# Attention in a two-layer trunk: the denominators' selection issued three steps later, and a buffer of its own for the transposed values

## The chip, the core and the metric

The kernel runs on one core of a Trainium2 chip. The metric is the device time of one execution in microseconds, lower is better; given is the median of three runs. One execution was also taken by the hardware profiler. Engines are named as in the profile: PE (TensorE, matmuls and transposes; PEld its weight loads), DVE (VectorE), ACT (ScalarE), POOL (GpSimd), SP (the queue that issues DMAs).

## What is computed

A trunk of two layers on 512 tokens of width 1024: a retention layer, then a layer of dilated attention, each followed by a gated MLP. The change lies in the attention layer. It has 16 heads of dimension 64 in three groups with (window, dilation) of (128, 1), (512, 4) and (2048, 16). Each group has its own queries, keys and values, and the groups' outputs are merged by their softmax denominators:

```python
s = jnp.where(valid, einsum('bqhd,bkhd->bhqk', qb, kb) * scale, -inf)
m = jnp.max(s, axis=-1, keepdims=True)
p = jnp.exp(s - m)
den = jnp.sum(p, axis=-1)
o = einsum('bhqk,bkhd->bqhd', p, vb) / den
lse = m[..., 0] + jnp.log(den)
...
alpha = softmax(stack(lses), axis=0)          # over the three groups
o = einsum('gbsh,gbshd->bshd', alpha, stack(outs))
```

Because the groups are merged by these weights, the kernel adds up the unnormalised outputs of all groups under one common maximum and divides once by the sum of all denominators.

## The kernel before

**Projections.** Keys, queries and values are projected in fp32 split into a high and a low part, three matmuls for each product (`mm3`, lines 208 to 210). Each projection of 128 columns (`rotated` for keys and queries, `residue_values` for the values of groups 1 and 2, `values` for those of group 0) is a Python generator. It yields after every `mm3` of its eight, so one *step* is three matmuls of 512 columns. Weights are fetched by SP into `raw`, scaled by a gain on POOL (L158), split by ACT (`whi`, L168) and DVE (`wlo`, L169).

**Heads.** `heads(hp, ...)` treats two heads at a time, so there are eight *pairs* (hp = 0 to 7). A query block of 128 rows has an index rb: 0 to 3 are the four blocks of group 0 in token order, 4 to 7 the four residues modulo 4 that serve groups 1 and 2. The stages are:

- scores in two halves (L756, `sc`): rb 0 to 3 with group 0, then rb 4 to 7 with groups 1 and 2; DVE adds the mask and takes row maxima (L760, `p` and `mst`);
- two *selections*, which bring the row maxima of the residue order into token order and back;
- exponentials with row sums `den` on ACT (L822);
- `weights(i, rb)`, steps i = 0 to 7 in the order rb = 4, 5, 6, 7, 0, 1, 2, 3, two at a time: PE transposes `p` into a bank of PSUM (`pt`, L846), and DVE for even i (L852) or ACT for odd i (L850) copies it out as `pT`. At i = 4 the first four are applied to the values (`apply`, L866, into `po`) ahead of the transposes of steps 4 and 5;
- a third selection, that of the denominators, and from it `inv`: one over the sum of all denominators, which ACT spreads (L885) and PE transposes (L895) to scale the output `o` (L896).

A selection is two functions. `select` spreads its source on DVE (L778, `spread`) and multiplies it by a 0/1 matrix on PE (L785, `pz`, 128x32, into a PSUM bank). `gather` reads `pz` on DVE (L790, `z`) and reduces it (L795); for the third selection a sum (L882) and a reciprocal (L883) follow.

**PSUM banks.** Tag "tr" has two banks, in turn used by half of the score tiles, by every `pt` and by `pz`. An instruction that writes into a bank waits until the tile that had it before is read. In the steps around the third selection the order of the tiles in "tr" is: `pt` of steps 2 and 3, `pz`, `pt` of steps 4, 5, 6 and 7, the output's `pt`.

**Order on the engines.** `_weave` drives a pair's `heads` generator, and at each of its `yield`s lets the filling generators (the next pair's projections) go on by 3.7 steps (hp 0, 1, 3, 5) or 2.95 (hp 2, 4, 6). PE's order is that of the program there (`manual_schedule`); the other engines' order is the scheduler's. The last pair (hp = 7) is woven with the output projection at one step per `yield`, and there PE's order is also the scheduler's.

**Residue values.** `residue_values` projects a value tile as 128 columns by 512 tokens; ACT copies it out in residue order to `vT` (L674), PE transposes it by residue (L693), and ACT copies the result to `vr` (L694). The transposes are issued some steps later (`transpose_pending`). `vT` is allocated under the tag "sh" with one buffer. The same tag and buffer serve `rotated` as scratch: DVE shuffles a projection into it (L714), POOL multiplies it (L717, L721) and adds it to the rotated tile `m` (L718, L722), which is a key or query tile of the next scores.

Of the kernel before, what the change touches and what calls it, by code (L numbers as in the profile page):

```python
# [10 lines left out]
F32 = mybir.dt.float32  # L11
# [6 lines left out]
P = 128  # L18
SEQ = 512
# [77 lines left out]
def trunk(ctx: ExitStack, tc: tile.TileContext, a, out):  # L97
# [95 lines left out]
    def cols_unit(w, n0, nt=1, k0=0, gain=None):  # L193
        return unit(cols_of(w, n0, nt, k0), gain)
# [11 lines left out]
    def mm3(o, l, r, start, stop):  # L206

        nc.tensor.matmul(o, lhsT=l[0], rhs=r[0], start=start, stop=False)  # L208
        nc.tensor.matmul(o, lhsT=l[0], rhs=r[1], start=False, stop=False)  # L209
        nc.tensor.matmul(o, lhsT=l[1], rhs=r[0], start=False, stop=stop)  # L210
# [402 lines left out]
    def attention(pool, post, then, late, ahead):  # L613
# [5 lines left out]
        def by_residue(t):  # L619
            return t.rearrange("p (q r) -> p r q", r=4)  # L620

        def in_runs(t):
            return t.rearrange("p (r q) -> p r q", r=4)

        with pool as tmp:
# [37 lines left out]
            def residue_values(hp, g, res):  # L663


                pm = ps.tile([P, 512], F32, name="pm", tag="mm", bufs=4)
                wu = cols_unit(w_kv, 3 * D + g * D + hp * P, gain=g_kv)
                for k in range(KT):
                    mm3(pm, [t[:, blk(k)] for t in wu], (hi[:, k, :], lo[:, k, :]), k == 0, k == KT - 1)
                    aged(k)  # L670
                    if k < KT - 1:
                        yield
                vT = tmp.tile([P, SEQ], F32, name="vT", tag="sh", bufs=1)
                nc.scalar.copy(out=in_runs(vT), in_=by_residue(pm))  # L674
                v = rtiles[hp % 2 * 2 + g - 1]
                pending.append([vT, v, 0])
                res.append(v)
                yield

            def aged(k):  # L680

                for t in pending:
                    t[2] += 1
                if k == 6:
                    transpose_pending(0)
# [45 lines left out]
            def heads(hp, ks, qs, vs, vr, res):  # L731
# [43 lines left out]
                def select(src, m_in, mat):  # L775

                    spread = small.tile([P, 4, 8], F32, name="spread", tag="spread", bufs=2)
                    nc.vector.tensor_mul(  # L778
                        out=spread,
                        in0=src.unsqueeze(1).broadcast_to([P, 4, 8]),  # L780
                        in1=m_in.unsqueeze(2).broadcast_to([P, 4, 8]),
                    )
                    pz = ps.tile([P, 512], F32, name="pz", tag="tr")
                    spread = spread.rearrange("p i c -> p (i c)")
                    nc.tensor.matmul(pz[:, 0:32], lhsT=mat, rhs=spread, start=True, stop=True)  # L785
                    return pz
# [47 lines left out]
                def weights(i, rb):  # L834


                    if rb < 4:
                        src = [sc[rb][:, :, 0:P] if rb == 0 else sc[rb][:, :, P:]]
                        if rb < 3:
                            src.append(sc[rb + 1][:, :, 0:P])  # L840
                    else:
                        src = [sc[rb][:, :, 0:P], sc[rb][:, :, P:]]
                    pt = ps.tile([P, 2, 2, P], F32, name="pt", tag="tr")
                    for h in range(2):
                        for n, p in enumerate(src):
                            nc.tensor.transpose(out=pt[:, h, n, :], in_=p[:, h, :], identity=ident)  # L846
                    pT = tmp.tile([P, 2, 2, P], F32, name="pT", tag="pT", bufs=6)
                    n = len(src)
                    if i % 2:
                        nc.scalar.copy(out=pT[:, :, 0:n, :], in_=pt[:, :, 0:n, :])  # L850
                    else:
                        nc.vector.tensor_copy(out=pT[:, :, 0:n, :], in_=pt[:, :, 0:n, :])  # L852
                    return pT, n

                def apply(i, rb, pT, n):

                    for g in range(1 if rb < 4 else 2):
                        for h in range(2):
                            hs = slice(h * HD, (h + 1) * HD)
                            if rb < 4:  # L860
                                v, p = vs[rb][:, hp % 2, hs], pT[:, h, 0:n, :].rearrange("p n q -> p (n q)")
                                dst = po[hs, rb * P : (rb + n) * P]
                            else:
                                v, p = vr[g][:, rb - 4, hs], pT[:, h, g, :]
                                dst = row_cols(po[hs, :], rb)
                            nc.tensor.matmul(dst, lhsT=v, rhs=p, start=i == 0 and g == 0, stop=i == 7)  # L866
# [3 lines left out]
                for i in range(0, 8, 2):  # L870
                    if i == 4:
                        for t in prev:
                            apply(*t)
                    prev += [(j, order[j], *weights(j, order[j])) for j in (i, i + 1)]
                    if i == 2:
                        pz = select(den[:, 8:16], quarter, sel[:, 0:128])
                    yield
                    yield

                inv = small.tile([P, 8], F32, name="inv", tag="inv", bufs=2)  # L880
# [50 lines left out]
            for hp in range(last + 1):  # L931
                att = heads(hp, *kq[hp], vs[hp // 2], vr[hp], o)
                if hp == last:
                    _weave(att, wo, 1)
                    _run(wo)
                    break

                fill = [residue_values(hp + 1, g, vr[hp + 1]) for g in (1, 2)] + [keys_queries(hp + 1, *kq[hp + 1])]
                if hp == 0:
                    fill = [residue_values(0, g, vr[0]) for g in (1, 2)] + fill  # L940
                if hp % 2 == 1:
                    fill.append(values(hp // 2 + 1, vs[hp // 2 + 1]))
                fill = chain(*fill)
                with tc.manual_schedule(engines={E.PE}):
                    _weave(att, fill, 3.7 if hp % 2 or hp == 0 else 2.95)
                    _run(fill)
                if hp == last - 1:
                    for _ in range(6):
                        next(wo)
# [65 lines left out]
```

## Time and profile before

| | |
|---|---|
| time, median of three runs | 1747.56 us (1743.99 to 1750.2) |
| the profiled execution's own time | 1750.31 us |
| its span in the profile | 1748.5 us |
| mean granted clock of PE | 0.991 |
| HBM read, written | 152.62 MB, 2.10 MB |
| heads and their fill, 845 to 1347 us: PE, DVE, ACT, POOL busy | 487.65, 284.95, 184.42, 265.16 of 502 us |

Times in the profile count from the start of the span. A timeline's row has start, duration, engine, line, operation, the tiles as out<-in, the shape, a count, and in brackets how long the engine had been idle and what released it. Matmuls are pipelined, so their rows overlap: the distance of two starts is what one costs. In the table of waits stand the instruction that waited, what it waited for, the total, the number of times and the longest. The row of a window has, in this order, its bounds, its length, the busy time and the number of instructions (in brackets) of PE, PEld, DVE, ACT and POOL, the granted clock of PE, the busy share of the DMA engines and GB/s.

### The profile page before, as it was taken

Reading aid. Unit: us, or ns where it says so; the run is one execution under the profiler, and the core shown is the slowest. Engines: PE = TensorE matmul, PEld = TensorE weight load, DVE = VectorE, ACT = ScalarE, POOL = GpSimd, SP = SyncE. Lnnn points to the kernel's source line nnn. Section 1 sums busy time; section 2 is a strip of 40 time slices with the busy share of each in tenths; the row PEclk is TensorE's granted clock in tenths of the full one; section 3 lists DMA queues with packets and bytes.
Section 4 is the critical chain, followed back from the end, with each engine's and each line's share of the span. In section 5 each row is a group of like instructions: output and inputs, shape, how many; then the busy total and the mean of one; then the engine's idle time right before and its main releaser. Section 6 shows DMA issues by size and latency. Waiting matters only on the chain.

```text
span 1748.5 us, 21650 instructions
## 1 busy us (share of the span) xinstructions
PE 1709.0 (98%) x8590; PEld 1417.3 (81%) x8590; DVE 939.2 (54%) x1461; ACT 613.3 (35%) x1076; POOL 397.5 (23%) x284
## 2 busy tenths in 40 slices
PE   9999999999999999999899999999999999999998
PEld 6888888887888888878778888878887788888886
DVE  4553545468544544557546556556455754454454
ACT  5232422325442422423144243244245544233241
POOL 1000000005000000046665656566431400000003
PEclk9999999999999999999999999999999999999999
DMA  6422333214332332432222222222221333233231
GB/s 211 125 67 84 91 97 91 85 36 109 121 96 73 121 96 73 133 106 61 85 71 64 85 73 81 68 70 85 69 73 44 87 116 97 83 111 96 84 109 49
DMA packets 202162, 156.10 MB, mean 89 GB/s; under 512 B 4989, under 2 KB 182093, under 8 KB 202062
## 3 DMA queue, kind: packets, MB, share of 16 engines
q1 hardware_dynamic: 202062, 154.73, 28.9%
q8 instruction: 67, 1.10, 0.3%
q14 instruction: 33, 0.27, 0.0%
HBM read 152.62 MB, written 2.10 MB: 88 GB/s over the span
## 4 chain that ended last, share of the span: by engine, by line
PE 89%; DVE 5%; POOL 3%; ACT 1%; issue 1%; DMA 1%; POOLq 0%; SPq 0%; DVEq 0%; ACTq 0%
PE pm L208 20%; PE pm L210 20%; PE pm L209 20%; PE po L208 6%; PE po L209 6%; PE po L210 6%; PE sc L756 2%; DVE wlo L169 2%; PE po L866 2%; PE pt L846 1%; DVE x L305 1%; PE s L450 1%; PE pt L264 1%; DVE h L256 1%; POOL raw L158 1%
## 5 line engine op out<-in xcount | busy, mean ns | idle before, releaser
L208 PE MATMUL pm<-hT_hi,whi 128*128 128x512 f32 (+1 forms) x1424 | 546.3, 384 | 0.0
L209 PE MATMUL pm<-hT_lo,whi 128*128 128x512 f32 (+1 forms) x1424 | 540.0, 379 | 0.3 <-DVE hT_lo L199 0.3
L210 PE MATMUL pm<-hT_hi,wlo 128*128 128x512 f32 (+1 forms) x1424 | 539.7, 379 | 0.0
L169 DVE TENSOR_TENSOR wlo<-raw,whi 128x1024 fp32r<-128x1024 f32 x275 | 377.7, 1378 | 299.9 <-ACT whi L168 296.2
L168 ACT CAST whi<-raw 128x1024 fp32r<-128x1024 f32 x275 | 286.0, 1051 | 650.0 <-PE pm L209 355.3
L208 PEld LDWEIGHTS pm<-hT_hi,whi 128*128 128x128 f32 x1424 | 269.6, 189 | 51.5 <-issue 3.2
L210 PEld LDWEIGHTS pm<-hT_hi,wlo 128*128 128x128 f32 x1424 | 269.3, 189 | 50.1
L209 PEld LDWEIGHTS pm<-hT_lo,whi 128*128 128x128 f32 x1424 | 269.6, 189 | 48.5 <-DVE hT_lo L199 1.2
L158 POOL TENSOR_TENSOR raw<-raw,cols 128x1024 f32<-128x1024 f32 x72 | 140.7, 1957 | 465.8 <-DMA raw<-in_att_w_kv 385.6
L271 DVE TENSOR_TENSOR m<-po,m 128x512 f32<-128x512 f32 x112 | 77.1, 688 | 139.0 <-PE po L210 138.8
L208 PE MATMUL pm<-whi,hT_hi 128*128 128x512 f32 (+1 forms) x384 | 142.2, 370 | 0.0
L323 POOL TENSOR_TENSOR h<-m,gain 128x512 f32<-128x512 f32 x31 | 47.4, 1528 | 407.7 <-DVE m L271 407.2
L208 PE MATMUL po<-whi,ah 128*128 128x512 f32 x352 | 137.9, 392 | 0.0
L209 PE MATMUL po<-wlo,ah 128*128 128x512 f32 x352 | 137.9, 392 | 0.0
L210 PE MATMUL po<-whi,al 128*128 128x512 f32 x352 | 137.8, 391 | 0.0
L210 PE MATMUL pm<-whi,hT_lo 128*128 128x512 f32 (+1 forms) x384 | 136.9, 356 | 0.0
L209 PE MATMUL pm<-wlo,hT_hi 128*128 128x512 f32 (+1 forms) x384 | 136.7, 356 | 0.0
L215 POOL TENSOR_TENSOR r_gn<-v_gn,nhalf 128x1 f32<-128x1 f32 x16 | 8.8, 548 | 357.4 <-DVE v_gn L480 357.4
L208 PEld LDWEIGHTS pm<-whi,hT_hi 128*128 128x128 f32 x384 | 73.0, 190 | 11.5 <-issue 1.0
L209 PEld LDWEIGHTS pm<-wlo,hT_hi 128*128 128x128 f32 x384 | 73.1, 190 | 10.8 <-DVE wlo L169 0.6
L210 PEld LDWEIGHTS pm<-whi,hT_lo 128*128 128x128 f32 x384 | 72.8, 190 | 10.7 <-DVE hT_lo L199 0.3
L208 PEld LDWEIGHTS po<-whi,ah 128*128 128x128 f32 x352 | 66.5, 189 | 14.2 <-DVE m L271 0.4
(137 smaller groups left out, 1959.8 us busy)
## 6 DMA issues: line engine op xcount, KB each, us to landing
raw<-in_ffn_w_up SPq DMA_DIRECT2D x88, 512.0 KB, 3.8
raw<-in_att_w_kv SPq DMA_DIRECT2D x48, 512.0 KB, 4.0
raw<-in_ret_w_in SPq DMA_DIRECT2D x47, 512.0 KB, 3.9
raw<-in_ffn_w_down SPq DMA_DIRECT2D x44, 512.0 KB, 3.2
raw<-in_att_w_q SPq DMA_DIRECT2D x24, 512.0 KB, 3.7
raw<-in_ret_w_out SPq DMA_DIRECT2D x16, 512.0 KB, 3.3
raw<-in_att_w_o SPq DMA_DIRECT2D x8, 512.0 KB, 3.3
x<-in_x SPq DMA_DIRECT2D x3, 512.0 KB, 6.6
```

The source lines that it names most:

```text
L158: nc.gpsimd.tensor_mul(out=dst, in0=dst, in1=gain.unsqueeze(2).broadcast_to(list(src.shape)))
L168: nc.scalar.copy(out=hi, in_=raw)
L169: nc.vector.tensor_sub(out=lo, in0=raw, in1=hi.bitcast(F32))
L208: nc.tensor.matmul(o, lhsT=l[0], rhs=r[0], start=start, stop=False)
L209: nc.tensor.matmul(o, lhsT=l[0], rhs=r[1], start=False, stop=False)
L210: nc.tensor.matmul(o, lhsT=l[1], rhs=r[0], start=False, stop=stop)
L256: nc.vector.scalar_tensor_tensor(out=h, in0=x[b][:, half(c)], scalar=r, in1=gain[c], op0=ALU.mult, op1=ALU.mult)
L264: nc.tensor.transpose(out=pt[:, j, :], in_=hs[c][:, blk(j)], identity=ident)
L271: nc.vector.tensor_add(out=dst, in0=src, in1=dst)
L323: eng.tensor_mul(out=mg[b][c], in0=m[b][:, half(c)], in1=gain[:, half(c)])
L756: nc.tensor.matmul(pm[h][:, i, c], lhsT=q, rhs=k, start=True, stop=True)
L866: nc.tensor.matmul(dst, lhsT=v, rhs=p, start=i == 0 and g == 0, stop=i == 7)
```

## The change

```diff
                 # residue_values
-                vT = tmp.tile([P, SEQ], F32, name="vT", tag="sh", bufs=1)
+                vT = tmp.tile([P, SEQ], F32, name="vT", tag="vT", bufs=1)
                 nc.scalar.copy(out=in_runs(vT), in_=by_residue(pm))
...
                 # heads, the loop over i in range(0, 8, 2)
                     prev += [(j, order[j], *weights(j, order[j])) for j in (i, i + 1)]
-                    if i == 2:
+                    yield
+                    if i == 4:
                         pz = select(den[:, 8:16], quarter, sel[:, 0:128])
-                    yield
                     yield
```

The selection of the denominators is issued at i = 4, after one of the two `yield`s, instead of at i = 2 ahead of both: three `yield`s later. In "tr" the order of tiles becomes `pt` of steps 2, 3, 4 and 5, `pz`, `pt` of steps 6 and 7. `vT` gets 2 KB per partition of its own; the order on ACT, POOL and SP is the same as before. ACT's copy into `vT` then no longer waits for POOL (in before, the first `vT` of hp 0, 1, 3 and 5 did).

On PE, in the first pair, the selection leaves the place behind the transposes of steps 2 and 3 and goes to one behind those of steps 4 and 5. The difference against before:

```order
@@ -3840,5 +3840,4 @@
 L210 MATMUL pm<-hT_hi,wlo 128x512
 L846 MATMUL pt<-ident,p 128x128 x8
-L785 MATMUL pz<-spread,sel 128x32
 L208 MATMUL pm<-hT_hi,whi 128x512
 L209 MATMUL pm<-hT_lo,whi 128x512
@@ -3883,4 +3882,5 @@
 L209 MATMUL pm<-hT_lo,whi 128x512
 L210 MATMUL pm<-hT_hi,wlo 128x512
+L785 MATMUL pz<-spread,sel 128x32
 L208 MATMUL pm<-hT_hi,whi 128x512
 L209 MATMUL pm<-hT_lo,whi 128x512
```

In between lie eight steps, `apply` for the first four tiles, the transposes of steps 4 and 5, and three steps; the next transposes, those of step 6, come three or four steps behind the new place (six in hp 1, 3 and 5). The same holds in hp 1 to 6, with six steps in place of the eight in hp 2, 4 and 6. In the last pair the selection goes behind the transposes of steps 4 and 5 and two matmuls.

On DVE, the reading of `pz` and what follows from it move behind the copy of step 4 (the first L852 below). In hp 2, 4 and 6 they also move behind the handling of a finished projection (L714, L716) and a weight's low part (L169):

```order
+L852 COPY pT<-pt 128x512
+L714 STREAM_SHUFFLE sh<-pm 128x512
+L716 TENSOR_TENSOR m_79<-pm,rope 128x512
+L169 TENSOR_TENSOR wlo<-raw,whi 128x1024
 L790 TENSOR_TENSOR z<-pz,sel 128x32
 L795 TENSOR_REDUCE inv<-z 128x8
 L882 TENSOR_TENSOR inv<-inv,den 128x8
 L883 RECIPROCAL inv<-inv 128x8
-L852 COPY pT<-pt 128x512
-L714 STREAM_SHUFFLE sh<-pm 128x512
-L716 TENSOR_TENSOR m_79<-pm,rope 128x512
-L169 TENSOR_TENSOR wlo<-raw,whi 128x1024
```

In hp 0, 1, 3 and 5 they stand directly behind the copy of step 4.

## The prediction

> **What bounds the kernel now.** I read the page first, then who waited for whom on PE, then the places of these waits in the timeline, and the granted clock around them. In the page's part 1, a column is an engine's busy time and its share of the span; its part 4 gives the shares of the chain that ended last. The table of waits has the waiting instruction, its releaser, the total in us, the number of times, the longest.
>
> ```profile
> PE 1709.0 (98%) x8590; PEld 1417.3 (81%) x8590; DVE 939.2 (54%) x1461; ACT 613.3 (35%) x1076; POOL 397.5 (23%) x284
> PE 89%; DVE 5%; POOL 3%; ACT 1%; issue 1%; DMA 1%; POOLq 0%; SPq 0%; DVEq 0%; ACTq 0%
> PE pt L264 <- DVE h L256: 9.9, 7, 2.0
> PE pz L785 <- DVE pT L852: 9.3, 7, 2.0
> PE pt L693 <- ACT vT L674: 5.0, 1, 5.0
> ACT whi L168 <- PE pm L209: 355.3, 123, 6.8
> ```
>
> PE is the bound: whatever it idles is added to the time, and whatever other engines idle is not. Weights do not limit it: ACT's split of a weight tile waited 123 times for PE to hand a buffer back, so the weights stand ready ahead of PE. Of PE's few waits the change touches two: 9.3 us before the third selection (`pz`, L785), one wait in each of seven pairs of heads, and 5.0 us before the first transposes of residue values (L693).
>
> **The selection's wait.** First pair of heads (the first five rows), and the seventh (the next three). The last two rows are eight transposes followed by no selection.
>
> ```profile
> 895.46 1.04 PE L846 MATMUL pt<-ident,p 128*128 128x128 f32 x8
> 895.99 1.89 DVE L169 TENSOR_TENSOR wlo<-raw,whi 128x1024 fp32r<-128x1024 f32 x1 [0.56 <-ACT whi L168]
> 897.80 0.68 DVE L852 COPY pT<-pt 128x512 f32<-128x512 f32 x1
> 898.53 0.41 PE L785 MATMUL pz<-spread,sel 128*128 128x32 f32 x2 [2.04 <-DVE pT L852]
> 898.78 0.48 PE L208 MATMUL pm<-hT_hi,whi 128*128 128x512 f32 x1
> ...
> 1289.55 1.03 PE L846 MATMUL pt<-ident,p 128*128 128x128 f32 x8
> 1291.54 0.41 PE L785 MATMUL pz<-spread,sel 128*128 128x32 f32 x2 [0.95 <-DVE pT L852]
> 1291.78 0.48 PE L208 MATMUL pm<-hT_hi,whi 128*128 128x512 f32 x1
> ...
> 961.74 1.04 PE L846 MATMUL pt<-ident,p 128*128 128x128 f32 x8
> 962.53 0.48 PE L208 MATMUL pm<-hT_hi,whi 128*128 128x512 f32 x1
> ```
>
> The two banks of the tag "tr" go round. `pz` stands directly behind the transposes of steps 2 and 3 and takes the bank of step 2, which DVE has still to copy out; DVE is in a weight's `wlo` (1.89 us) and begins the copy 2.3 us after the transposes began. PE stands still, in order. Without a selection the next projection starts 0.79 us after the eight transposes (961.74 to 962.53). Here it starts 3.32 us after them, 2.53 too late, and in the seventh pair 2.23, 1.44 too late. So the delay is the listed wait plus 0.49 in the first and in the last of the seven.
>
> **What the move does to it.** It puts `pz` three steps (nine projection matmuls) behind the transposes of steps 4 and 5. It then takes the bank of step 4. The rows are of the third pair, whose DVE queue is the worse one after the change:
>
> ```profile
> 1038.11 1.09 PE L846 MATMUL pt<-ident,p 128*128 128x128 f32 x8
> 1038.80 0.69 DVE L852 COPY pT<-pt 128x512 f32<-128x512 f32 x1 [4.00 <-PE pt L846]
> 1038.96 0.47 PE L208 MATMUL pm<-hT_hi,whi 128*128 128x512 f32 x1
> 1039.27 0.39 PE L209 MATMUL pm<-hT_lo,whi 128*128 128x512 f32 x1
> 1041.11 0.39 PE L208 MATMUL pm<-hT_hi,whi 128*128 128x512 f32 x1
> 1041.25 1.97 DVE L169 TENSOR_TENSOR wlo<-raw,whi 128x1024 fp32r<-128x1024 f32 x1
> 1043.15 0.82 PE L846 MATMUL pt<-ident,p 128*128 128x128 f32 x6
> ...
> 951.29 0.30 PE L785 MATMUL pz<-spread,sel 128*128 128x32 f32 x2
> 951.43 0.48 PE L208 MATMUL pm<-hT_hi,whi 128*128 128x512 f32 x1
> 951.74 0.39 PE L209 MATMUL pm<-hT_lo,whi 128*128 128x512 f32 x1
> ```
>
> The copy of step 4 waited for PE (4.00 us) and was done at 1039.49; nine matmuls later, at 1041.11, `pz` would find its bank free 1.6 us ago. No wait is left there. What stays is a selection alone between projections: 0.14 us to the next start, and 0.31 instead of 0.23 to the one after (a 0.23 step is (1041.11 - 1039.27) / 8), together 0.22. Gain per pair: wait + 0.49 - 0.22, so over seven 9.3 + 7 x 0.27 = **11.2 us**. The upper bound of this term is 9.3 + 7 x 0.49 = 12.7 (a selection that costs nothing), the lower one comes with the first rival. The eighth pair had no such wait; its `pz` will stand behind step 5's transposes and two matmuls, and I put it at nothing, between -0.5 and +0.5.
>
> The new wait that the move adds: `pz` holds its bank until DVE's `z` (L790) has read it, and the transposes of step 7 want that bank. On DVE in the third, fifth and seventh pair `z` now stands behind the `wlo` above, which ends at 1041.25 + 1.97 = 1043.22; `z` (0.19 us in its rows) is done near 1043.45. PE starts step 6's transposes at 1043.15 + 0.22, step 7's four 0.11 us transposes later, at 1043.81. It is hidden with 0.36 us to spare. In the other pairs `z` follows the copy of step 4 directly and DVE waits for PE. What queues behind `z` (the reduction, sum and reciprocal, 0.6 to 1.8 us, then the copy of step 6) is wanted by the output transposes six or more steps later; that covers it, and if it did not, the price would be what is over 4 us. DMA queues and POOL keep their order.
>
> **The clock behind the waits.** Each row is one stretch: its bounds, its length, busy time and count of PE, PEld, DVE, ACT and POOL, then the granted clock.
>
> ```profile
> 896.29:899.70 3.41, 1.37 (x8) 1.03 (x7) 2.84 (x5) 0.58 (x1) 3.41 (x3) 1.00 0.18 47
> 899.70:903.11 3.41, 3.41 (x10) 2.63 (x9) 1.39 (x2) 0.00 (x0) 3.41 (x3) 0.50 0.37 111
> 1094.26:1097.67 3.41, 1.60 (x12) 1.19 (x10) 3.41 (x3) 0.58 (x1) 3.41 (x2) 1.00 0.00 0
> 1097.67:1101.08 3.41, 3.18 (x15) 2.67 (x16) 1.72 (x5) 0.00 (x0) 1.99 (x2) 1.00 0.53 154
> 1227.38:1230.79 3.41, 3.41 (x10) 2.64 (x10) 1.53 (x4) 0.00 (x0) 1.96 (x3) 0.50 0.53 154
> ```
>
> After two of the three 2 us waits PE ran 3.41 us at half clock; after the third, whose idle time was split over two stretches (1.60 us busy against 1.37), it did not. Half of 3.41 is lost: 1.7 each, **3.4 us** in this execution, and it goes with the waits; zero if another execution's stretches fall otherwise. [...]
>
> **The transposed values' buffer.** ACT's `vT` shared one buffer ("sh") with the rotation's scratch and so waited for POOL's last read of it:
>
> ```profile
> 853.29 1.06 ACT L168 CAST whi<-raw 128x1024 fp32r<-128x1024 f32 x1 [6.36 <-PE pm L209]
> 855.07 0.39 PE L210 MATMUL pm<-hT_hi,wlo 128*128 128x512 f32 x1
> 858.23 1.51 POOL L722 TENSOR_TENSOR m<-m,sh 128x512 f32<-128x512 f32 x1
> 859.78 0.58 ACT L674 COPY vT<-pm 128x512 f32<-128x512 f32 x1 [5.43 <-POOL m L722]
> 860.41 1.11 PE L693 MATMUL pt<-ident,vT 128*128 128x128 f32 x4 [4.96 <-ACT vT L674]
> 861.46 3.79 PE L756 MATMUL sc<-m 64*128 64x128 f32 x32
> ```
>
> With its own buffer `vT` follows the cast, done near 854.93, and the transposes run near 855.5. But the whole 5 us are not won: behind them stand the second half's scores, and these read the query tile `m` that the same POOL instruction finishes at 859.74. Only the first four of the 32 records (group 1) can go earlier. The other 28 begin near 859.8 instead of 861.46 + 4 x 3.79/32 = 861.9, or somewhat later: **2.2 us** earlier, with the clock at half in both. Bounds: 0 (POOL itself later) and 5.0 (if scores could go at once). The later uses of `vT` were not waited for.
>
> **The sum.** 11.2 + 3.4 + 2.2 = 16.8. The profiled execution took 1750.31 (span 1748.5), so 1733.5; it lies 2.75 above the median of the three runs shown (1747.56), and part of that can be the clock. From the median with half of the clock's term, 11.2 + 1.7 + 2.2 = 15.1, comes 1732.5. I predict **1733**, and take a run's share within 0.3% (5 us) as no change.
>
> **Rivals.**
> - The wait moves to step 7's transposes. `wlo` takes 1.89 and 1.97 us above; were it a microsecond longer, `z` would be 0.64 too late for PE in three pairs, 1.9 in all; with a buffer that gives nothing and no clock's part the gain is 11.2 - 1.9 = 9.3, or 1738. For it: the margin is 0.36 us. Against: `wlo` must stretch in each.
> - The clock comes out otherwise: the half-clock stretches are elsewhere or stay. In this execution 1750.31 - 13.4 = 1737, from the median 1734; also faster.
> - No change: PE is paid out of the wait and stopped by what DVE delivers late. Then only the 2.2 remain, 1745. For it: `pz` waited because DVE was late. Against: the next to want that copy are the weighted sums after eight steps, 5.5 us at 0.69, where the copy was late by 2.04.
> - Slower: the bank. `pz` in one of two banks, and `z` behind DVE's queue: PE's cover is three steps, `pz` and four transposes, 2.7 us. If `z` came over 5 us after `pz` in all eight pairs, PE would lose 2.7 x 8 = 21 us or more against 16.8 won: 1752. It decides from 2.7 + 16.8/8 = 4.8 us. Against: DVE has 0.36 us or more to spare.
>
> **Numbers.** The forecast 0.74, the moved wait 0.10, the clock 0.07, no change 0.06, slower 0.03. Faster by over 0.3% then has 0.91, within 0.3% 0.06, slower 0.03. The range goes from the lowest run shown, 1743.99, less 16.8 (1727) to the first rival's 1738 and the 3 us by which runs lie above the median: 1741.
>
> **What would show it.** In the profile after: no row "PE pz <- DVE pT" among PE's waits; `pz` between projections; clock 1.00 in the stretches behind steps 2 and 3; ACT's `vT` near 855 and the scores waiting for POOL's L722 instead. I am wrong if PE's waits name DVE's `z` or `pT` with several us, if weights (`wlo`) appear among them, or if PE's idle time falls and the span does not.

## The result, and the profile after

The changed kernel took 1733.22 us in the median of six runs (1730.73 to 1739.26), the kernel before 1746.38 in the median of six, the three of the table above among them (1742.76 to 1750.2): a ratio of 0.9931, 95% interval 0.9907 to 0.9955. The forecast was 1733 in a range of 1727 to 1741. The profiled execution after took 1731.12 (span 1729.3, clock 0.997), that of before 1750.31.

The page after, part 1 and the first line of part 4, and then, from the table of waits, all rows of the heads:

```profile
PE 1699.7 (98%) x8590; PEld 1409.3 (81%) x8590; DVE 932.0 (54%) x1461; ACT 613.7 (35%) x1076; POOL 400.2 (23%) x284
PE 91%; DVE 3%; POOL 2%; issue 1%; DMA 1%; ACT 1%; POOLq 0%; SPq 0%; DVEq 0%; ACTq 0%
PE sc L756 <- POOL sh L721: 2.3, 1, 2.3
PE sc L756 <- POOL m L722: 1.1, 1, 1.1
PE pt L693 <- DVE mst L760: 0.5, 1, 0.5
```

The same 8590 matmuls keep PE busy for 1699.7 us where it was 1709.0: at half clock it was busy for 6.70 us where it was 24.42, and half of that difference, 8.9, is nearly all of the 9.3. The chain still runs through PE, its share up from 89% to 91%, and DVE's down from 5% to 3%. The row of `pz` with 9.3 us is gone, the 5.0 us before L693 are 0.5, and the scores now wait (by the table for POOL). A row for a weight, `PE pm L209 <- DVE wlo L169` with 0.5 us, which the prediction would have taken for a sign against it, lies ahead of the heads, where nothing was changed.

The 19.2 us between the two profiled executions fall in three places, read from the starts of the same instructions in both. Ahead of the heads there are 3.7 us, where nothing was changed: the one of before ran at half clock in three more stretches there (13.65 us, against 3.41). Behind the heads there is nothing (403.68 against 403.73). The heads took 498.87 before and 483.32 after, 15.55 less, by pairs (from the first scores, then from output transpose to output transpose, L895):

| pair | 1 | 2 | 3 | 4 | 5 | 6 | 7 | 8 |
|---|---|---|---|---|---|---|---|---|
| before | 77.79 | 69.05 | 58.38 | 70.74 | 58.38 | 72.33 | 58.40 | 33.80 |
| after | 72.36 | 68.45 | 57.21 | 68.45 | 57.21 | 68.45 | 57.21 | 33.96 |
| won | 5.43 | 0.60 | 1.17 | 2.28 | 1.17 | 3.88 | 1.18 | -0.16 |

Before, pairs 2, 4 and 6 had the same work and three different lengths; after, they agree to 0.01.

**The selection at its new place.** The timeline after: PE and DVE in the first pair, where `pz` stands behind the transposes of steps 4 and 5, and then in the third pair.

```profile
898.57 1.09 PE L846 MATMUL pt<-ident,p 128*128 128x128 f32 x8
900.04 0.68 DVE L852 COPY pT<-pt 128x512 f32<-128x512 f32 x1
901.57 0.30 PE L785 MATMUL pz<-spread,sel 128*128 128x32 f32 x2
901.71 0.48 PE L208 MATMUL pm<-hT_hi,whi 128*128 128x512 f32 x1
901.91 0.19 DVE L790 TENSOR_TENSOR z<-pz,sel 128x32 f32<-128x32 f32 x1 [1.20 <-PE pz L785]
...
1029.96 0.30 PE L785 MATMUL pz<-spread,sel 128*128 128x32 f32 x2
1030.11 2.12 DVE L169 TENSOR_TENSOR wlo<-raw,whi 128x1024 fp32r<-128x1024 f32 x1
1032.16 0.18 DVE L790 TENSOR_TENSOR z<-pz,sel 128x32 f32<-128x32 f32 x1
1032.26 0.82 PE L846 MATMUL pt<-ident,p 128*128 128x128 f32 x6
```

In the first pair the copy ends at 900.72 and `pz` runs at 901.57, without a bracket, so without a wait; the next projection starts 0.14 us later, the figure that the prediction took. In the third pair `z` does stand behind a weight's `wlo` and ends at 1032.34; step 7's transposes, 0.44 us into the last row, start at 1032.70. That leaves 0.36 us, the figure forecast, although this `wlo` took 2.12 us. The exact figure is luck: `wlo` was 0.15 us longer, but `z` followed it 0.12 sooner and the transposes came 0.04 later than in the prediction's working. A second profile of the same kernel leaves 0.24 us in this pair.

**The clock around it.** A window after, over the steps on both sides of the old place and of the new:

```profile
889.00:903.00 14.00, 14.00 (x96) 11.71 (x95) 8.22 (x13) 3.29 (x4) 13.73 (x8) 1.00 0.38 110
```

PE is busy in all 14.00 us at clock 1.00, where before it stood for 2.04 us and then ran 3.41 us at half.

**The transposed values.** Timeline after, first pair:

```profile
850.54 0.58 ACT L674 COPY vT<-pm 128x512 f32<-128x512 f32 x1
852.24 0.63 PE L693 MATMUL pt<-ident,vT 128*128 128x128 f32 x4 [0.48 <-DVE mst L760]
852.87 2.24 POOL L721 TENSOR_TENSOR sh<-sh,rope 128x512 f32<-128x512 f32 x1
854.95 0.08 DVE L760 DVE_READ_ACCUMULATOR2_ANT mst<- 128x1 f32 x1
855.17 0.49 PE L756 MATMUL sc<-m 64*128 64x128 f32 x4 [2.30 <-POOL sh L721]
855.19 1.51 POOL L722 TENSOR_TENSOR m<-m,sh 128x512 f32<-128x512 f32 x1
856.76 2.96 PE L756 MATMUL sc<-m 64*128 64x128 f32 x28 [1.10 <-POOL m L722]
```

ACT copies `vT` directly behind its cast (L168, from 849.59, 1.05 us), and the transposes wait 0.48 us where they waited 4.96. The second half's scores are then held twice. The last 28 of the 32 wait 1.10 us for L722, as the prediction had it. Ahead of that the first four wait 2.30 us, which it did not have. The profile names L721 as what came last, but no score reads what L721 writes (the scratch `sh`), and the tile that these four read was finished by the L722 before it, at 849.59. What they lacked was, by the program, the bank: their `sc` takes the bank of "tr" that DVE's row maxima (the row of `mst`) free near 855.02, 0.09 us before L721 ends. In all four profiles with `vT` in its own buffer and no work moved ahead these two ends lie 0.09 us apart, so no run here separates them. Of 5.0 us waited, 0.48 + 2.30 + 1.10 = 3.9 were waited again, by this reading 2.8 of them for a bank and 1.1 for POOL.

### The profile page after: what moved, and what is told of

Its sections match the earlier page's. It is cut to its first block, busy times and chain, and to the rows that moved or that the text cites. A ratio compares the mean times of both kernels' runs of the same rounds, so it can differ in the third digit from the quotient of the medians.

```text
span 1729.3 us, 21643 instructions
## 1 busy us (share of the span) xinstructions
PE 1699.7 (98%) x8590; PEld 1409.3 (81%) x8590; DVE 932.0 (54%) x1461; ACT 613.7 (35%) x1076; POOL 400.2 (23%) x284
## 4 chain that ended last, share of the span: by engine, by line
PE 91%; DVE 3%; POOL 2%; issue 1%; DMA 1%; ACT 1%; POOLq 0%; SPq 0%; DVEq 0%; ACTq 0%
PE pm L208 21%; PE pm L210 21%; PE pm L209 21%; PE po L208 6%; PE po L209 6%; PE po L210 6%; PE sc L756 2%; PE po L866 2%; PE pt L846 2%; DVE x L305 1%; PE s L450 1%; DVE h L256 1%; PE pt L264 1%; PE y L208 1%; PE y L209 1%
## 5 line engine op out<-in xcount | busy, mean ns | idle before, releaser
L209 PE MATMUL pm<-hT_lo,whi 128*128 128x512 f32 (+1 forms) x1424 | 538.0, 378 | 0.1
L169 DVE TENSOR_TENSOR wlo<-raw,whi 128x1024 fp32r<-128x1024 f32 x275 | 372.7, 1361 | 299.8 <-ACT whi L168 296.3
L168 ACT CAST whi<-raw 128x1024 fp32r<-128x1024 f32 x275 | 286.0, 1051 | 642.4 <-PE pm L209 331.3
L209 PEld LDWEIGHTS pm<-hT_lo,whi 128*128 128x128 f32 x1424 | 268.3, 188 | 47.9 <-DVE hT_lo L199 1.0
L158 POOL TENSOR_TENSOR raw<-raw,cols 128x1024 f32<-128x1024 f32 x72 | 144.1, 2003 | 453.7 <-DVE m L271 314.0
L209 PE MATMUL po<-wlo,ah 128*128 128x512 f32 x352 | 137.4, 390 | 0.0
L209 PE MATMUL pm<-wlo,hT_hi 128*128 128x512 f32 (+1 forms) x384 | 136.4, 355 | 0.5 <-DVE wlo L169 0.5
L209 PEld LDWEIGHTS pm<-wlo,hT_hi 128*128 128x128 f32 x384 | 72.8, 190 | 11.4 <-DVE wlo L169 1.2
```

The costliest lines, as they stand in the source:

```text
L158: nc.gpsimd.tensor_mul(out=dst, in0=dst, in1=gain.unsqueeze(2).broadcast_to(list(src.shape)))
L168: nc.scalar.copy(out=hi, in_=raw)
L169: nc.vector.tensor_sub(out=lo, in0=raw, in1=hi.bitcast(F32))
```

## The experiments

Diffs are against the changed kernel or the kernel before, as each says; the one with eleven steps is shown against the one with eight. Lengths of pairs are read as in the table above. "First pair" is here counted from an earlier instruction that is the same in all kernels (a transpose, L264, 36.7 us ahead of the first scores) to the first output transpose, because some kernels move work ahead of these scores: 114.51 us before, 109.08 after.

**The selection alone.** The changed kernel with `vT` back in its old buffer:

```diff
-                vT = tmp.tile([P, SEQ], F32, name="vT", tag="vT", bufs=1)
+                vT = tmp.tile([P, SEQ], F32, name="vT", tag="sh", bufs=1)
```

> The third selection moved as in the change, vT still in the buffer of tag sh. Theory A (the bank: the gain is the seven waits of the third selection, with the half-clock stretches behind some of them): no row 'PE pz <- DVE pT' is left, the 5.0 us wait of L693 for vT stays, and the time is 11 to 15 us below before, 1732 to 1736. Rival B (most of the gain is the buffer of vT): 2 us below before, 1744.

Measured: 1734.57 us against 1745.87, ratio 0.9932 (0.9913 to 0.9951). Its table of waits has no row of `pz`, and of the two waits of the prediction only this is left:

```profile
PE pt L693 <- ACT vT L674: 5.0, 1, 5.0
```

Pairs 2 to 7 have the lengths of the changed kernel to 0.01 us (68.45 and 57.21), and the first pair 110.37. So the selection alone gives nearly all of the gain: theory A held, B did not.

**The buffer alone.** The kernel before with the first hunk of the change and not the second:

```diff
-                vT = tmp.tile([P, SEQ], F32, name="vT", tag="sh", bufs=1)
+                vT = tmp.tile([P, SEQ], F32, name="vT", tag="vT", bufs=1)
```

> vT in a buffer of its own, the third selection at its old place. Theory A: the seven waits of pz stay (9.3 us), the wait of L693 falls from 5.0 us to under 1, but the scores behind it then wait 2 to 4 us for POOL; from the first scores to the first projection behind the second half of the scores 17.4 us instead of 19.2; time 1.8 us below before, 1744.5, within the noise. Rival B: the time falls by over 10 us, to about 1735.

Measured: 1744.72 us, ratio 0.9997 (0.9982 to 1.0012). Its waits:

```profile
PE pz L785 <- DVE pT L852: 5.8, 7, 1.9
PE sc L756 <- POOL sh L721: 2.0, 1, 2.0
PE sc L756 <- POOL m L722: 1.1, 1, 1.1
```

The wait at L693 is gone and turned into 3.1 us of the scores' waits. From the first scores to the first projection behind the second half it took 17.11 us, where 17.4 was expected. In time the buffer's gain of some 2 us cannot be told from nothing here, with an interval of 0.3%; a main part of the gain, which B gave it, is excluded. That the waits of `pz` came to 5.8 us and not to 9.3 was expected by neither theory: in pairs 4 and 6 it waited 0.35 us instead of 2.03. Two later runs ask why.

**The old place, another bank.** The kernel before with the third selection's `pz` in a bank of the tag that the weighted sums use:

```diff
-                def select(src, m_in, mat):
+                def select(src, m_in, mat, tag="tr"):
...
-                    pz = ps.tile([P, 512], F32, name="pz", tag="tr")
+                    pz = ps.tile([P, 512], F32, name="pz", tag=tag)
...
-                        pz = select(den[:, 8:16], quarter, sel[:, 0:128])
+                        pz = select(den[:, 8:16], quarter, sel[:, 0:128], "po")
```

> The kernel before, with one edit: at its old place the third selection writes into a bank of tag po instead of tr. PE's order is that of before. Theory A (PE waits for the bank that DVE has not copied out): the waits of pz vanish although it stands where it stood, and the time is as in the run with the selection moved, 1732 to 1736. Rival C (the place is what costs: its source or its neighbours, or DVE being late in any case): pz still waits about 9 us in all, or the wait reappears at the next transposes, and the time stays at 1746.

Measured: 1735.64 us, ratio 0.9934 (0.9915 to 0.9952). First pair, timeline:

```profile
895.94 1.03 PE L846 MATMUL pt<-ident,p 128*128 128x128 f32 x8
896.81 0.31 PE L785 MATMUL pz<-spread,sel 128*128 128x32 f32 x2
898.26 0.68 DVE L852 COPY pT<-pt 128x512 f32<-128x512 f32 x1
```

`pz` runs 1.45 us before the copy that it used to wait for has begun. DVE is as late as ever and it costs nothing; pairs 2 to 7 take 68.44 and 57.20 us. What PE waited for was the bank and nothing else: neither the denominators nor DVE's work behind `pz`. A held, C did not.

**One `yield` later.** The kernel before with the selection still at i = 2 but behind the first `yield`, so that it still takes the bank of step 2, behind three or four steps of cover:

```diff
-                    if i == 2:
-                        pz = select(den[:, 8:16], quarter, sel[:, 0:128])
                     yield
+                    if i == 2:
+                        pz = select(den[:, 8:16], quarter, sel[:, 0:128])
                     yield
```

> The kernel before with the third selection one yield later (behind steps 2 and 3 and four projection steps, three in pairs 3, 5 and 7) instead of three yields; it still takes the bank of step 2, and vT keeps the buffer of tag sh. Theory A (only cover is needed): the copy of step 2 was late by at most 2.04 us against 2.1 to 2.7 us of cover, so the waits of pz fall below 1 us in all and the time is that of the selection moved by three yields, about 1734.5. Rival F (it must leave the bank of step 2, or stand behind the weighted sums): 4 us or more of waits stay, time 1739 or more.

Measured: 1734.62 us against 1748.16, ratio 0.9924 (0.9909 to 0.9939). No row of `pz` among the waits. First pair:

```profile
895.91 1.03 PE L846 MATMUL pt<-ident,p 128*128 128x128 f32 x8
898.45 0.68 DVE L852 COPY pT<-pt 128x512 f32<-128x512 f32 x1
899.54 0.30 PE L785 MATMUL pz<-spread,sel 128*128 128x32 f32 x2
```

The copy is done at 899.13, 0.41 us before `pz`. So the distance to the copy is what counts, and a third of the change's move is enough for it: A held, F did not.

**What is left in the first pair.** The changed kernel waits there for 0.5 + 2.3 + 1.1 us. The idea is that PE comes to these places too early, with too little filling work ahead of them. Eight steps of it are put ahead of the first pair, and the rest is spread more thinly:

```diff
+                    if hp == 0:
+                        _take(fill, 8)
-                    _weave(att, fill, 3.7 if hp % 2 or hp == 0 else 2.95)
+                    _weave(att, fill, 3.3 if hp == 0 else 3.7 if hp % 2 else 2.95)
```

> The changed kernel, with eight steps of the first pair's filling projections ahead of its first scores, and 3.3 instead of 3.7 steps at each later yield of that pair, so that the same projections are issued. Theory D (what is left in the first pair is POOL's last rotation, 3.9 us of PE waits with 3.4 us at half clock behind them): the rows of L693 and L756 vanish from PE's waits and the time falls by 4 to 5.5 us below the changed kernel, to about 1728.5. Rival E (that pair is held by POOL and the weights whatever PE does first): the waits turn up elsewhere, at wlo or the next vT, and the time is that of the changed kernel, 1733.

Measured: 1732.48 us, ratio 0.991 (0.9887 to 0.9932). In the profile the first pair took 105.61, 3.5 us less than after; the median time is only 0.7 us below the changed kernel's 1733.22, where 4 to 5.5 were expected, and that is within the noise. One wait stayed, larger than it was, and the timeline shows what came before it:

```profile
854.73 4.92 DVE L169 TENSOR_TENSOR wlo<-raw,whi 128x1024 fp32r<-128x1024 f32 x2
860.56 0.63 PE L693 MATMUL pt<-ident,vT 128*128 128x128 f32 x4 [2.24 <-DVE mst L760]
```

DVE had two weights ahead of the row maxima that release the transposes' bank. So theory D held in part: the rows of L756 vanished, that of L693 did not, and DVE's weights had a share in it beside POOL's rotation. With more steps ahead, PE comes there later:

```diff
-                        _take(fill, 8)
-                    _weave(att, fill, 3.3 if hp == 0 else 3.7 if hp % 2 else 2.95)
+                        _take(fill, 11)
+                    _weave(att, fill, 3.2 if hp == 0 else 3.7 if hp % 2 else 2.95)
```

> The changed kernel with eleven steps of the first pair's fill ahead of its first scores and 3.2 steps at each later yield of that pair. Theory D: 2.2 us of the run with eight steps stayed because DVE came to the row maxima only after two weights; three steps more cover that and POOL's last rotation, so no wait over 0.5 us is left in the first pair, its length with what stands ahead of it is 5 to 6 us below that of the changed kernel at the same clock, and the time is near 1728.5. Rival E: new waits of 2 us or more at vT, at row maxima or at wlo, time 1731 to 1733.

Measured: 1730.84 us, ratio 0.9899 (0.9881 to 0.9916), and no row of the heads left among PE's waits: D held there, though the time lay 2.3 us above its 1728.5, and this round alone does not set it apart from the changed kernel. Run once more, together with the changed kernel unchanged:

> The changed kernel, unchanged, on the same chip as the next one. Both theories: a ratio to before of 0.992 to 0.994, about 1733. Clock theory: the executions fall into levels some 1.7 us apart per half-clock stretch, from about 1731 with a granted clock of 0.997 to about 1739 with 0.991.

> Eleven steps of the first pair's fill ahead of its first scores, once more, beside the changed kernel on one chip. Theory D: 4 to 6 us below the changed kernel, ratio to before 0.989 to 0.991. Rival E: within 2 us of the changed kernel, the difference seen so far being the clock's.

Measured: the changed kernel 1733.78 us (1730.98 to 1741.05), ratio 0.9944 (0.9923 to 0.9966), just above the 0.992 to 0.994 expected; the eleven steps 1725.31 (1724.87 to 1731.12), ratio 0.9894 (0.9877 to 0.991). The first pair, whole, in the changed kernel (first row, the execution shown above) and with eleven steps ahead (second, from this round):

```profile
805.53:914.61 109.08, 105.20 (x600) 88.65 (x601) 63.08 (x102) 36.13 (x69) 72.74 (x39) 0.98 0.29 83
805.59:909.41 103.82, 103.82 (x603) 87.85 (x604) 66.59 (x102) 36.22 (x69) 72.85 (x39) 1.00 0.30 87
```

PE is busy in 105.20 of 109.08 us at clock 0.98, and with eleven steps in all of 103.82 at 1.00: 5.26 us less, of which 3.88 are idle time and the rest the clock. The second pair is another 0.70 shorter (67.75 against 68.45), since more of the filling work is done by then. The medians differ by 8.5 us here, more than the 4 to 6 expected: D held, E did not. The two executions profiled in this round lie 9.4 us apart, and there what goes beyond these 6.0 is for the most part the clock's: 1.80 us of it stand ahead of the heads and 2.09 behind them, where the programs do not differ, and the changed kernel ran at half clock for one stretch more in each place (from 411.70 and from 1346.95). The kernel with eleven steps is the fastest measured here.

**Why 5.8 and not 9.3.** The kernel before and the one with the buffer alone, each profiled again:

> The kernel before, unchanged, for another profile. Theory G (whether DVE's weight or POOL's multiplication in the fourth and sixth pair starts first is a matter of some 0.1 us and so differs between executions): pz waits in these pairs are 0.35 or 2.03 us by chance, the total between 5.8 and 9.3. Rival H (it is set by the program; vT's own buffer shortened them): again 2.03 in both and 9.3 in all.

> vT in a buffer of its own alone, for another profile. Theory G: the waits of pz in the fourth and sixth pair are 0.35 or 2.03 us by chance. Rival H: again 0.35 in both and 5.8 in all.

Measured: 1745.86 and 1747.85 us, one run each. The waits of `pz` in the first, then in the second:

```profile
PE pz L785 <- DVE pT L852: 9.4, 7, 2.2
```

```profile
PE pz L785 <- DVE pT L852: 9.5, 7, 2.2
```

The same program with the buffer alone gave 5.8 us in one execution and 9.5 in the other. The fourth pair, DVE and POOL, in the first of them and then in the second:

```profile
1092.15 1.21 DVE L169 TENSOR_TENSOR wlo<-raw,whi 128x1024 fp32r<-128x1024 f32 x1
1092.19 2.93 POOL L158 TENSOR_TENSOR raw<-raw,cols 128x1024 f32<-128x1024 f32 x1 [0.76 <-DMA raw<-in_att_w_kv]
```

```profile
1093.34 1.90 POOL L158 TENSOR_TENSOR raw<-raw,cols 128x1024 f32<-128x1024 f32 x1 [0.66 <-DMA raw<-in_att_w_kv]
1093.39 2.94 DVE L169 TENSOR_TENSOR wlo<-raw,whi 128x1024 fp32r<-128x1024 f32 x1
```

The one that starts first, by 0.04 or 0.05 us, takes 1.21 (DVE) or 1.90 us (POOL); the other takes 2.93 (POOL) or 2.94 (DVE). When DVE came second, `pT` was late and `pz` waited 2.04 us in that pair instead of 0.35. In the sixth pair, too, DVE came first where `pz` waited 0.34 us, and second where it waited 2.0. The second profile of before fits both theories; that of the buffer alone fits G and not H. So the two waits went with which engine started first, and POOL's start came behind a weight's DMA (0.76 and 0.66 us of idleness). The kernel before has the same order of work there and may have executions with short waits too, but its two profiles both show some 2 us.

## Why the prediction was right, step by step

- **The wait goes and none takes its place** (11.2 us): right, and its causes are shown. It was the bank (another bank at the old place does the same), and the cover (one `yield` does the same). Wait + 0.27 for a pair says 0.62, 1.22, 2.30, 1.22, 2.30 and 1.22 for pairs 2 to 7, before the clock; measured are 0.60, 1.17, 2.28, 1.17, 3.88 and 1.18. The eighth pair, put at nothing within 0.5, lost 0.16.
- **The rival of the moved wait**: its place was right and it did not come; the room left in the third, fifth and seventh pair was 0.24 to 0.51 us in the two profiles of the changed kernel. "No change" and "slower" fell with it; DVE's lateness did not turn up behind `pz`.
- **The clock behind the waits** (3.4 us): right in kind and size in the profiled execution. The sixth pair won 3.88, which is 1.6 more than the fourth with the same wait. In the first pair, what follows the second half's scores won 3.60, where 4.0 was forecast; 0.3 of the difference is the half-clock stretch behind the scores' own wait, which reached 0.99 us into this part after and 0.39 before. That it would be different in other executions was said, and it is so: the four profiles of kernels with these waits (before and the buffer alone, twice each) have 2, 1, 0 and 0 half-clock stretches behind them, 1.3 us on average, less than the 1.7 that the prediction took for its median. Clocks of the changed kernel's twelve runs go from 0.990 to 0.997, and their times from 1741.05 to 1730.73 in the same order; that they lie on levels 1.7 us apart is not shown.
- **The buffer** (2.2 us, 2.1 by its own figures): the last condition (L722) right, the term a little large, and the wait for the bank ahead of it not foreseen. From the first scores to the first projection behind the second half's scores it took 19.23 us before and 17.40 after: 1.83. The 28 scores went 1.59 us earlier (856.76, where 862.05 less the 3.70 of the earlier start of the heads makes 858.35): POOL's last addition ended 0.66 us later against the work around it (856.70 against 859.74 - 3.70 = 856.04), a case that the prediction had named ("or somewhat later") and not priced. About half of that, 0.35, stood already at POOL's addition before it. The other 0.24 of the 1.83 is the clock's, which was not at half "in both": after, these scores began 0.47 us ahead of the half-clock stretch. Over the nine profiles with no work moved ahead, this part took 19.15 to 19.48 us in the five without the buffer and 16.94 to 17.80 in the four with it, some 2 us less. In the median of runs the buffer's part is not shown.
- **The sum**: 16.8 forecast in the heads of the profiled execution, 15.55 measured there. Its total came out 2.4 us below the 1733.5 expected of it, through the 3.7 us ahead of the heads, which no step had. Against the medians the gain is smaller than the 15.1 taken: over all runs here, 45 of before and 12 after, 1745.87 - 1733.22 = 12.65. That 1733 was met to 0.2 us is luck: the three runs shown of before lay 1.7 above that median, so a gain sized 2.4 too large came off a start 1.7 too high, and the rounding up of 1732.5 did the rest. The interval of the result, 8 to 16 us, does not exclude 15.1; the clock's average share is the part that I would now take lower.

## What to carry to other kernels

When a small matmul waits, ask which bank it takes, who had that bank, and how much of PE's own work lies between that tile's last matmul and this one; here a bank elsewhere or a few matmuls of cover removed the waits (9.3 us), and what DVE did late then cost nothing. Before pricing a removed wait, look for the next condition of what stands behind it: here 3.9 of 5.0 us were waited again. And ask of the instruction that a profile names whether the waiting one reads anything of it: the wait may be for a bank. Gaps left in a PE-bound stage can be closed by moving filling work ahead of them (5.3 us in the first pair here), and a wait with a half-clock stretch behind it was worth 1.6 us more than the same wait without one (3.88 us in the sixth pair, 2.28 in the fourth).

## What the runs showed of the hardware

**Half clock came in stretches of 3.41 us.** In the profile of before the granted clock was 0.50 from 411.59, 428.66, 899.70 and 1227.38 for 3.41 us each, and from 783.65 and 858.74 for 6.83; in the one after from 782.14 and 857.23 for 3.41. In both, one more begins behind the last matmuls (1742.79 and 1724.22) and runs to the end. Within each profile the starts lie whole multiples of 3.413 us apart, as 899.70 and 1227.38 do by 96 of them; they fall elsewhere in the other profile. The same wait of 2.03 us (L264, behind the heads) in the kernel with eight steps ahead, with the stretch after it, and then in the changed kernel, split by the bounds of its rows, which lie 142 to 144 times 3.413 us behind 857.23 to 0.1 us, into 1.87 and 0.16 us:

```profile
1343.73:1347.14 3.41, 1.38 (x11) 1.11 (x11) 3.06 (x4) 0.57 (x1) 3.00 (x4) 1.00 0.53 154
1347.14:1350.55 3.41, 3.41 (x11) 2.67 (x10) 3.41 (x4) 2.55 (x8) 1.86 (x2) 0.50 0.00 0
```

```profile
1341.99:1345.41 3.42, 1.55 (x7) 0.94 (x5) 2.58 (x2) 0.76 (x3) 3.11 (x4) 1.00 0.39 115
1345.41:1348.82 3.41, 3.25 (x18) 2.75 (x19) 3.41 (x5) 2.41 (x6) 2.79 (x3) 1.00 0.13 38
```

With 2.03 us of idleness in the first row (3.41 less 1.38) the second runs at half clock; with 1.87 and 0.16 (3.42 less 1.55, 3.41 less 3.25) both rows stay at full. In the profile of before, 2.04 us stood ahead of the half-clock stretch at 899.70 and 2.03 ahead of that at 1227.38, while behind the 1.81 us of 1094.26 to 1097.67 the clock stayed at full. One case goes the other way: ahead of the half clock from 783.65 there were only 1.76 us, of a wait of 2.96 that ran on into it. What decides the clock these rows do not show.

**DVE and POOL: in three executions the one that started later took longer.** The rows above have 1.21 and 2.94 us for the same DVE instruction (L169) and 1.90 and 2.93 for the same POOL instruction (L158). The later one ended 2.97 and 2.99 us after the start of the first, near the 3.11 that the two short times add up to. The fourth pair of before has it too: POOL from 1094.26 took 1.90 us, DVE from 1094.33 took 2.91. POOL had waited for a transfer in the rows above (0.76 and 0.66 us), so by them a transfer's arrival stood behind a matmul's wait two engines away, 0.35 or 2.04 us.
